# HGRN2 recurrence in a two-layer decoder trunk: 128-column products cut into two of 64, merged decays, a later output step

## The chip, the cores and the metric

The kernel runs on one NeuronCore of a Trainium2 chip. The metric is the device time of one execution in microseconds; a kernel's time is the median over its runs. TensorE multiplies into PSUM (128 partitions, banks of 512 float32 columns); VectorE (DVE in the profile), ScalarE (ACT) and GpSimd (POOL) do the rest; SyncE (SP) issues most transfers.

## The reference, cut to what matters

Two layers of a trunk at sequence length 256 and width 2048. Layer 0 holds a chunked gMLP beside an HGRN2 recurrence with 8 heads of 128, layer 1 an attention; a gated feed-forward follows each. The change touches the HGRN2 heads alone:

```python
def hgrn2(q, f_logit, i, g, lower_bound, o_gain):
    log_f = jnp.logaddexp(jnp.log(lb), jnp.log1p(-lb) + jax.nn.log_sigmoid(fl))
    k = (1.0 - lb) * jax.nn.sigmoid(-fl)
    ...
    def step(state, xs):
        q_c, k_c, v_c, lf_c = xs
        G = jnp.cumsum(lf_c, axis=2)
        o_inter = jnp.einsum('bhtk,bhkv->bhtv', q_c * jnp.exp(G), state)
        ...
        decay = jnp.exp(jnp.where(mask[:, :, None], diff, -jnp.inf))
        scores = jnp.einsum('bhtk,bhtsk,bhsk->bhts', q_c, decay, k_c)
        o_intra = jnp.einsum('bhts,bhsv->bhtv', scores, v_c)
        ...
    o = rms_norm(o, o_gain) * jax.nn.silu(g.astype(f32).reshape(shp))
```

For a pair of tokens t >= s, a head's score is the sum over features of q[t], k[s] and the product of the forget gates from s + 1 to t.

## The kernel before

All weights are streamed from HBM, split into two parts (`wh` on ScalarE, L168; `wl` on VectorE, L169) and multiplied in three matmuls a tile: L285 to L287 (`project_tok`), L259 and L262 (`project`), L304 to L306 (`project_four`). Everything between these products is written as generators. `tick()` (L121) is called once for each chunk of weights and moves every generator in flight on by one `yield`; up to `depth[0]` of them are in flight, three during the recurrence. So the order of the work is: a chunk of weights and its matmuls, then a step of each generator.

`mixer_ab` (L469) runs the projections of layer 0 one after another: v, f, then for each of 8 heads q (L750), with the values i in two groups of four heads (`values`, called ahead of heads 3 and 6), then the gates g and u. `gates` (L596) makes a head's forget gates `l` (128 features x 256 tokens; the second half of the tokens in reverse order) and keys `t[:, 0]`, `t[:, 1]`; L751 and L752 put the queries into `t[:, 3]` and `t[:, 2]`. Each head then runs `hgrn(h)` (L630):

- The diagonal of the scores: two products of 128 x 128 (L639), multiplied with an identity into the state tile `st` (L640). `st[:, 0]` holds the first 128 tokens' scores, `st[:, 1]` the last 128 tokens'.
- The levels (L648): for block widths n = 1, 2, 4, ... 64 from fine to coarse, ScalarE copies the decayed keys and queries into `E` (L652, two copies a level), then VectorE multiplies the even blocks (L656) and the odd blocks (L658) with the decay of their neighbour and folds the decays `tot` (L660). The last level (64) has only the even blocks.
- The scores of the levels: one product of 128 x 128 for each of the seven (L669), four into one PSUM bank and three into another, with the product between the two halves of the sequence (L673) between; VectorE copies each level's blocks into `st` under a mask (L682), after four levels and after the rest.
- The outputs, when the group's values exist (`itoks`): three products (L695 to L697), then a norm.

float32 products have two instructions each on TensorE. `tied` (L627) holds a product back until the matmul issued last by a projection; beyond that the instructions of an engine stand in an order that the framework chooses. PSUM tiles of the recurrence come from four banks (`px`).

Of the kernel before, what the change touches and what calls it, by code (L numbers as in the profile page):

```python
# [8 lines left out]
F32 = mybir.dt.float32  # L9
F32R = mybir.dt.float32r  # L10
U16 = mybir.dt.uint16
AF = mybir.ActivationFunctionType
ALU = mybir.AluOpType
AX = mybir.AxisListType

P = 128
S = 256
# [35 lines left out]
def tile_trunk(ctx: ExitStack, tc: tile.TileContext, x, pp_d, cst_d, mlev_d, msk_d,  # L53
# [13 lines left out]
    def nm(base):  # L67
        count[0] += 1
        return f"{base}_{count[0]}"
# [21 lines left out]
    def act(out_, in_, func, **kw):  # L91
        name = TABLE.get(func)
        if name is not None and name != epoch["set"]:
            ld = SC.preload_act_table_set(name)
            for o in epoch["ops"]:
                tc.add_manual_dep(ld.ins, o.ins.name, order, reason="table order")
            epoch.update(set=name, load=ld, ops=[ld])
        r = SC.activation(out_, in_, func, **kw)
        if name is not None:
            tc.add_manual_dep(r.ins, epoch["load"].ins.name, order, reason="table order")  # L100
            epoch["ops"].append(r)
        return r

    def view(ap, off, *dims):
        return bass.AP(ap.tensor, ap.offset + off, [list(ap.ap[0])] + [list(d) for d in dims])

    def back(ap):
        return view(ap, P - 1, (-1, P))
# [5 lines left out]
    def bank(tag="px"):  # L114
        n = nm(tag)
        return px.tile([P, 512], F32, tag=tag, name=n, bufs=banks[tag])

    banks = {"px": 4}
    flight, queue = [], []

    def tick():  # L121
        while queue and len(flight) < depth[0]:
            flight.append(queue.pop(0))
        for g in list(flight):
            if next(g, flight) is flight:
                flight.remove(g)
# [342 lines left out]
    def mixer_ab(norm):  # L469
# [126 lines left out]
        def gates(j, z):  # L596

            for _ in range(LAG):
                yield
            for i in range(4):  # L600
                l = keep("lf")
                t = hp.tile([P, 4, P], F32, tag="two", name=nm("kq"), bufs=2 * NH)
                first, second = view(z, i * S, (2, P)), view(z, (i + 1) * S - 1, (-2, P))
                held(act(l[:, 0:P], first, AF.Sigmoid))
                act(l[:, P:S], second, AF.Sigmoid)
                act(t[:, 0], first, AF.Sigmoid, scale=-1.0)
                act(t[:, 1], second, AF.Sigmoid, scale=-1.0)
                h = len(kq)
                V.tensor_scalar(t[:, 0:2], t[:, 0:2], omlb[:, h:h + 1], None, ALU.mult)
                lf.append(l)  # L610
                kq.append(t)
                yield
# [14 lines left out]
        def tied(r):  # L627
            tc.add_manual_dep(r.ins, deep["last"].ins.name, order, reason="not before")

        def hgrn(h):  # L630
            l, t = lf[h], kq[h]
            d0 = (h % 4) * P
            yield
            yield
            SC.activation(l, l, AF.Identity, bias=lb[:, h:h + 1], scale=omlb[:, h:h + 1])
            st = hp.tile([P, 2, P], F32, tag="st", name=nm("st"), bufs=3)
            dg = bank()
            for T in range(2):
                PE.matmul(dg[:, T * P:(T + 1) * P], t[:, T], t[:, 3 - T], start=True, stop=True)  # L639
            V.tensor_tensor(st, dg[:, 0:S].rearrange("p (a b) -> p a b", a=2),  # L640
                            ident.unsqueeze(1).to_broadcast([P, 2, P]), ALU.mult)
            yield

            V.tensor_tensor(t[:, 2:4], t[:, 2:4], view(l, P, (-P, 2), (1, P)), ALU.mult)
            E = hp.tile([P, NL, 2, P], F32, tag="E", name=nm("E"), bufs=2)
            tot = l
            tots = hp.tile([P, S], F32, tag="tot", name=nm("tot"), bufs=1)
            for li in reversed(range(NL)):  # L648
                n = LEVELS[li]
                m = P // n  # L650
                for sl in range(2):
                    SC.activation(E[:, li, sl].rearrange("p (b two n) -> p b two n", two=2, n=n),  # L652
                                  view(t, 2 * P * sl, (2 * n, 64 // n), (P + n, 2), (1, n)), AF.Copy)
                even = view(t, 0, (2 * P, 2), (2 * n, 64 // n), (1, n))
                odd = view(t, P + n, (2 * P, 2), (2 * n, 64 // n), (1, n))
                V.tensor_tensor(even, even, view(tot, 1, (m, 2), (2, m // 2), (0, n)), ALU.mult)  # L656
                if li:
                    V.tensor_tensor(odd, odd, view(tot, m, (-m, 2), (2, m // 2), (0, n)), ALU.mult)  # L658
                    nt = tots[:, S - 2 * m:S - m]
                    V.tensor_tensor(nt, view(tot, 0, (2, m)), view(tot, 1, (2, m)), ALU.mult)  # L660
                    tot = nt
                if n in (4, 16):
                    yield
            for _ in range(3):
                yield
            for c0, c1 in ((0, 4), (4, NL)):
                sps = bank()
                for li in range(c0, c1):
                    tied(PE.matmul(sps[:, (li - c0) * P:(li - c0 + 1) * P],  # L669
                                   E[:, li, 0], E[:, li, 1], start=True, stop=True))  # L670
                if c0 == 0:
                    xps = bank()
                    tied(PE.matmul(xps[:, 0:P], t[:, 0], t[:, 2], start=True, stop=True))  # L673
                    s128 = hp.tile([P, P], F32, tag="s128", name=nm("s128"), bufs=3)
                    SC.activation(back(s128), xps[:, 0:P], AF.Copy)
                for li in range(c0, c1):

                    n = LEVELS[li]
                    sv = view(st[:, 1], 0, (2 * n, 64 // n), (n - P, 2), (1, n))
                    m, d = (t_.rearrange("p (b two n) -> p b two n", two=2, n=n)  # L680
                            for t_ in (msk[:, li * P:(li + 1) * P], sps[:, (li - c0) * P:(li - c0 + 1) * P]))
                    V.copy_predicated(sv, m, d)  # L682
            s1 = hp.tile([P, P], F32, tag="s1", name=nm("s1"), bufs=2)
            SC.activation(back(s1), st[:, 1], AF.Copy)
            yield
            yield
            yield
            if len(itoks) <= h // 4:
                while len(itoks) <= h // 4:
                    yield  # L690
                yield
            itok = itoks[h // 4]
            op = bank()
            i0, i1 = (itok[:, T, d0:d0 + P] for T in range(2))
            tied(PE.matmul(op[:, 0:P], st[:, 0], i0, start=True, stop=True))  # L695
            tied(PE.matmul(op[:, P:S], s128, i0, start=True, stop=False))
            tied(PE.matmul(op[:, P:S], s1, i1, start=False, stop=True))  # L697
            so = hp.tile([P, LANE], F32, tag="so", name=nm("so"), bufs=2)[:, 0:2]
            ot = hp.tile([P, P], F32, tag="ot", name=nm("ot"), bufs=1)
            for T in range(2):  # L700
                SC.activation(ot, op[:, T * P:(T + 1) * P], AF.Square,
                              accum_out=so[:, T:T + 1])
            rsq(so, so, P)
            for T in range(2):
                SC.activation(os_[h // 4][:, T, d0:d0 + P], op[:, T * P:(T + 1) * P], AF.Copy,
                              scale=so[:, T:T + 1])
            left[0] -= 1
# [3 lines left out]
        def values(j):  # L711
            ps = project_tok(w_i[j], norm, lambda: hp.tile([P, 512], F32R, tag="ar", name=nm("ar"), bufs=2))
            itok = hp.tile([P, 2, 512], F32, tag="tok", name=nm("itok"), bufs=2)
            for T in range(2):
                SC.activation(itok[:, T], ps[T], AF.Copy, scale=Rr[:, T:T + 1])
            itoks.append(itok)

        silu = []

# [23 lines left out]
        for h in range(NH):  # L743
            if h in (3, 6):
                values(h // 4)
            while len(kq) <= h:
                tick()
            if h % 4 == 0:
                os_.append(hp.tile([P, 2, 512], F32, tag="o", name=nm("o"), bufs=2))
            z = fold(project(w_q[h], A))  # L750
            V.tensor_tensor(kq[h][:, 3], z[:, 0:P], R[:, 0:P], ALU.mult)  # L751
            V.tensor_tensor(back(kq[h][:, 2]), z[:, P:S], R[:, P:S], ALU.mult)  # L752
            queue.append(hgrn(h))
        for j in range(2):
            ps = project_four(w_g[4 * j:4 * j + 4], A, KT)
# [474 lines left out]
```

## Time and profile before

| | us |
|---|---|
| median of 3 runs (lowest to highest) | 2295.46 (2295.23 to 2295.96) |
| the profiled execution | 2295.65 |
| its span | 2293.9 |
| TensorE busy | 2288.2 |
| VectorE busy | 1566.4 |
| ScalarE busy | 1306.7 |
| GpSimd busy | 356.3 |

The profile shows each instruction with its engine, line and duration, groups of them by line, what an engine waited for, and the chain of work that ended last. PE is TensorE's matmuls and PEld its weight loads, which run beside the matmuls; matmul records overlap, so that a busy TensorE isn't one at its peak. Where a group is written `px<-E 128*128 128x128`, it reads tile `E`, writes a PSUM tile of pool `px`, uses 128 rows and 128 columns of the array, and moves 128 columns.

### The profile page before, as it was taken

To read this page: it belongs to the slowest core of one execution; us is meant where nothing else is said; L and a number is where in the kernel's file an instruction comes from. 1 tells how busy PE (TensorE), PEld (TensorE's weight loads), DVE (VectorE), ACT (ScalarE), POOL (GpSimd) and SP (SyncE) were. 2 spreads that over 40 slices of the span, in tenths; PEclk is the share of its full clock that TensorE was granted. 3 is DMA by queue.
4 is the path that set the end of the run, shared out by engine and by line. 5 is a ranking of instruction groups with operands and counts; after the bars stand their busy time and mean duration, and the time that the engine had idled before them with its cause. 6 is when DMAs were issued, how large, how long until landed. Compare 5 with 4: busy or idle time off the path is not lost.

```text
span 2293.9 us, 31385 instructions
## 1 busy us (share of the span) xinstructions
PE 2288.2 (100%) x10384; PEld 1902.4 (83%) x10384; DVE 1566.4 (68%) x2348; ACT 1306.7 (57%) x1964; POOL 356.3 (16%) x662
## 2 busy tenths in 40 slices
PE   9999999999999999999999999999999999999999
PEld 8888888888888888888888888888888888888887
DVE  7798767777566656766866665766776476657666
ACT  7676656665455545654555555655665465456642
POOL 0110212212012002111111101111211022012102
PEclk9999999999999999999999999999999999999999
DMA  8655677877667767776666656777777677667765
GB/s 290 197 156 157 196 217 226 242 214 229 199 206 218 213 200 210 221 216 187 211 222 202 194 178 179 224 221 235 228 223 215 194 215 211 211 202 218 222 203 174
DMA packets 489554, 480.38 MB, mean 209 GB/s; under 512 B 114128, under 2 KB 457184, under 8 KB 489392
## 3 DMA queue, kind: packets, MB, share of 16 engines
q1 hardware_dynamic: 467184, 453.54, 64.7%
q0 software_dynamic: 20480, 22.50, 4.4%
q10 hardware_dynamic: 1728, 2.35, 0.3%
q8 instruction: 81, 1.33, 0.3%
q14 instruction: 81, 0.66, 0.1%
HBM read 435.24 MB, written 2.11 MB: 191 GB/s over the span
## 4 chain that ended last, share of the span: by engine, by line
PE 98%; DMA 1%; DVE 1%; ACT 0%; issue 0%; SPq 0%; DVEq 0%; ACTq 0%
PE pm L305 26%; PE pm L304 26%; PE pm L306 26%; PE pm L285 4%; PE pm L286 4%; PE pm L287 4%; PE pm L259 2%; PE pm L186 1%; PE pm L262 1%; DMA w<-in_w_up 1%; PE pm L210 0%; PE px L669 0%; DVE wl L169 0%; PE px L888 0%; PE px L910 0%; ACT wh L168 0%
## 5 line engine op out<-in xcount | busy, mean ns | idle before, releaser
L169 DVE TENSOR_TENSOR wl<-w,wh 128x1024 fp32r<-128x1024 f32 (+1 forms) x820 | 996.0, 1218 | 630.3 <-ACT wh L168 620.7
L168 ACT ACTIVATE wh<-w 128x1024 fp32r<-128x1024 f32 (+1 forms) x820 | 862.3, 1054 | 791.4 <-PE pm L306 542.1
L304 PE MATMUL pm<-wh,a 128*128 128x512 f32 x1728 | 674.3, 390 | 0.0
L305 PE MATMUL pm<-wl,a 128*128 128x512 f32 x1728 | 672.6, 389 | 0.1
L306 PE MATMUL pm<-wh,a 128*128 128x512 f32 x1728 | 672.5, 389 | 0.0
L318 POOL DMA_DIRECT2D zt<-tmp x413 | 223.6, 549 | 1202.3 <-DVE tmp L313 1046.3
L305 PEld LDWEIGHTS pm<-wl,a 128*128 128x128 f32 x1728 | 324.4, 188 | 67.9 <-DVE wl L169 1.2
L306 PEld LDWEIGHTS pm<-wh,a 128*128 128x128 f32 x1728 | 324.3, 188 | 67.4
L304 PEld LDWEIGHTS pm<-wh,a 128*128 128x128 f32 x1728 | 324.4, 188 | 66.8
L304 PE MATMUL pm<-wh,hid 128*128 128x512 f32 x688 | 267.6, 389 | 0.0
L305 PE MATMUL pm<-wl,hid 128*128 128x512 f32 x688 | 267.6, 389 | 0.0
L306 PE MATMUL pm<-wh,hid 128*128 128x512 f32 x688 | 267.6, 389 | 0.0
L318 POOL DMA_DIRECT2D turn<-tmp x160 | 86.7, 550 | 506.3 <-DVE tmp L313 263.0
L285 PE MATMUL pm<-wh,a 128*128 128x512 f32 x416 | 165.2, 397 | 0.0
L287 PE MATMUL pm<-wh,a 128*128 128x512 f32 x416 | 162.2, 390 | 0.0
L286 PE MATMUL pm<-wl,a 128*128 128x512 f32 x416 | 162.0, 389 | 0.0
L306 PEld LDWEIGHTS pm<-wh,hid 128*128 128x128 f32 x688 | 129.1, 188 | 27.0
L304 PEld LDWEIGHTS pm<-wh,hid 128*128 128x128 f32 x688 | 129.1, 188 | 26.8
L305 PEld LDWEIGHTS pm<-wl,hid 128*128 128x128 f32 x688 | 129.1, 188 | 26.6
L1034 ACT ACTIVATE conv<-zt,pp 128x256 f32<-128x256 f32 x176 | 95.9, 589 | 26.2 <-DMA zt<-tmp 21.6
L313 DVE STREAM_TRANSPOSE tmp<-z 128x512 f32<-128x512 f32 x120 | 83.4, 704 | 19.4 <-ACT z L1020 18.7
L287 PEld LDWEIGHTS pm<-wh,a 128*128 128x128 f32 x416 | 78.1, 188 | 16.6
(241 smaller groups left out, 2097.7 us busy)
## 6 DMA issues: line engine op xcount, KB each, us to landing
w<-in_w_up SPq DMA_DIRECT2D x352, 512.0 KB, 4.5
w<-in_w_dn SPq DMA_DIRECT2D x176, 512.0 KB, 4.2
w<-in_w_cqkv SPq DMA_DIRECT2D x96, 512.0 KB, 4.4
w<-in_w_abo SPq DMA_DIRECT2D x32, 512.0 KB, 4.6
w<-in_w_cg SPq DMA_DIRECT2D x32, 512.0 KB, 4.3
w<-in_w_co SPq DMA_DIRECT2D x32, 512.0 KB, 4.6
zt<-tmp SPq DMA_DIRECT2D x414, 32.0 KB, 2.9
zt<-tmp POOLq DMA_DIRECT2D x413, 32.0 KB, 2.7
```

The source lines that it names most:

```text
L168: r = deep["wh"] = SC.activation(wh, w, AF.Copy)
L169: deep["wl"] = V.tensor_tensor(wl, w, wh.bitcast(F32), ALU.subtract)
L259: PE.matmul(ps, wh[:, k * P:(k + 1) * P], acts[done + k], start=done + k == 0, stop=False, skip_group_check=True)
L285: PE.matmul(ps[T], ah, h, start=k + i == 0, stop=False)
L286: PE.matmul(ps[T], ah, l, start=False, stop=False)
L287: deep["last"] = PE.matmul(ps[T], al, h, start=False, stop=k + i == KT - 1)
L304: PE.matmul(ps[T], ah, h, start=not begun and k + i == ks[0], stop=False)
L305: PE.matmul(ps[T], ah, l, start=False, stop=False)
L306: deep["mm"] = deep["last"] = PE.matmul(ps[T], al, h, start=False, stop=not more and k + i == ks[-1] + 1)
L313: V.transpose(tmp.rearrange("p (b m i t) -> p b m i t", b=4, m=4, t=2)[:, :, :, :, T], src(T).rearrange("p (m b j) -> p b m j", m=4, b=4))
L318: queues[(a + b) % len(queues)].dma_start(dst[BLK * b:BLK * (b + 1), :, a * n:(a + 1) * n], tmp[BLK * a:BLK * (a + 1), b * 4 * n:(b + 1) * ...
L1034: held(SC.activation(c, z, AF.Identity, bias=pp[:, cb:cb + 1], scale=w(2)))
```

## The change

- Diagonal and level products are each cut into two: rows 0 to 63 and 64 to 127 of the result, with 64 stationary and 64 moving columns each. A half is written into the upper or lower 64 PSUM partitions, and all seven levels now fit into one bank (7 x 64 columns). Blocks off the diagonal of 64, which no level below 64 needs, are no longer computed; level 64 takes the opposite column half.
- The masked copies become two a level, of 64 partitions and 64 columns each; level 64 is copied by ScalarE without a mask. The state tiles are three fixed ones whose never written quarters are set to zero once.
- The slots of `t` are permuted (keys in 0 and 3, queries in 2 and 1), so that the even blocks and the odd blocks of a level can be multiplied by one instruction of 256 elements instead of two of 128.
- A head's outputs are formed at the earliest two steps of `tick` after its values were made; before, a head that found them missing waited one step more, and one that found them went on at once.

```diff
+    steps = [0]
+
     def tick():
+        steps[0] += 1
...
-                act(t[:, 1], second, AF.Sigmoid, scale=-1.0)
+                act(t[:, 3], second, AF.Sigmoid, scale=-1.0)
                 h = len(kq)
-                V.tensor_scalar(t[:, 0:2], t[:, 0:2], omlb[:, h:h + 1], None, ALU.mult)
+                ks = view(t, 0, (3 * P, 2), (1, P))
+                V.tensor_scalar(ks, ks, omlb[:, h:h + 1], None, ALU.mult)
...
+        H = P // 2
+        sts = [hp.tile([P, 2, P], F32, tag=f"st{i}", name=f"st{i}") for i in range(3)]
+        for st in sts:
+            V.memset(st[H:P, 0, 0:H], 0.0)
+            V.memset(st[0:H, 1, H:P], 0.0)
...
-            st = hp.tile([P, 2, P], F32, tag="st", name=nm("st"), bufs=3)
+            st = sts[h % 3]
             dg = bank()
             for T in range(2):
-                PE.matmul(dg[:, T * P:(T + 1) * P], t[:, T], t[:, 3 - T], start=True, stop=True)
-            V.tensor_tensor(st, dg[:, 0:S].rearrange("p (a b) -> p a b", a=2),
-                            ident.unsqueeze(1).to_broadcast([P, 2, P]), ALU.mult)
+                for r in (0, H):
+                    PE.matmul(dg[r:r + H, T * H:(T + 1) * H], t[:, 3 * T, r:r + H], t[:, 2 - T, r:r + H],
+                              start=True, stop=True)
+            for r in (0, H):
+                V.tensor_tensor(st[r:r + H, :, r:r + H], dg[r:r + H, 0:P].rearrange("p (a b) -> p a b", a=2),
+                                ident[r:r + H, r:r + H].unsqueeze(1).to_broadcast([H, 2, H]), ALU.mult)
...
+                    two = P + n if sl else 3 * P + n
                     SC.activation(E[:, li, sl].rearrange("p (b two n) -> p b two n", two=2, n=n),
-                                  view(t, 2 * P * sl, (2 * n, 64 // n), (P + n, 2), (1, n)), AF.Copy)
-                even = view(t, 0, (2 * P, 2), (2 * n, 64 // n), (1, n))
-                odd = view(t, P + n, (2 * P, 2), (2 * n, 64 // n), (1, n))
-                V.tensor_tensor(even, even, view(tot, 1, (m, 2), (2, m // 2), (0, n)), ALU.mult)
+                                  view(t, P * sl, (2 * n, 64 // n), (two, 2), (1, n)), AF.Copy)
                 if li:
-                    V.tensor_tensor(odd, odd, view(tot, m, (-m, 2), (2, m // 2), (0, n)), ALU.mult)
+                    both = view(t, 0, (2 * P + n, 2), (2 * n, P // n), (1, n))
+                    V.tensor_tensor(both, both, view(tot, 1, (-1, 2), (2, m), (0, n)), ALU.mult)
...
+                else:
+                    even = view(t, 0, (P, 2), (1, n))
+                    V.tensor_tensor(even, even, view(tot, 1, (m, 2), (0, n)), ALU.mult)
...
-            for c0, c1 in ((0, 4), (4, NL)):
-                sps = bank()
-                for li in range(c0, c1):
-                    tied(PE.matmul(sps[:, (li - c0) * P:(li - c0 + 1) * P],
-                                   E[:, li, 0], E[:, li, 1], start=True, stop=True))
-                if c0 == 0:
-                    xps = bank()
-                    tied(PE.matmul(xps[:, 0:P], t[:, 0], t[:, 2], start=True, stop=True))
...
-                for li in range(c0, c1):
...
-                    V.copy_predicated(sv, m, d)
+            sps = bank()
+            for li in range(NL):
+
+                for r in (0, H):
+                    c = r if li else H - r
+                    tied(PE.matmul(sps[r:r + H, li * H:(li + 1) * H], E[:, li, 0, r:r + H], E[:, li, 1, c:c + H],
+                                   start=True, stop=True))
+            xps = bank()
+            tied(PE.matmul(xps[:, 0:P], t[:, 0], t[:, 1], start=True, stop=True))
+            s128 = hp.tile([P, P], F32, tag="s128", name=nm("s128"), bufs=3)
+            SC.activation(back(s128), xps[:, 0:P], AF.Copy)
+            for li in range(NL):
+
+                n = LEVELS[li]
+                for r in (0, H):
+                    d = sps[r:r + H, li * H:(li + 1) * H]
+                    if li == 0:
+                        SC.activation(st[r:r + H, r // H, H - r:P - r], d, AF.Copy)
+                        continue
+                    sv = view(st[r:r + H, 1], r, (2 * n, 32 // n), (n - P, 2), (1, n))
+                    m = msk[r:r + H, li * P + r:li * P + r + H]
+                    V.copy_predicated(sv, *(t_.rearrange("p (b two n) -> p b two n", two=2, n=n) for t_ in (m, d)))
...
-            if len(itoks) <= h // 4:
-                while len(itoks) <= h // 4:
-                    yield
-                yield
-            itok = itoks[h // 4]
+            while len(itoks) <= h // 4 or steps[0] < itoks[h // 4][1] + 2:
+                yield
+            itok = itoks[h // 4][0]
...
-            itoks.append(itok)
+            itoks.append((itok, steps[0]))
...
-            V.tensor_tensor(kq[h][:, 3], z[:, 0:P], R[:, 0:P], ALU.mult)
-            V.tensor_tensor(back(kq[h][:, 2]), z[:, P:S], R[:, P:S], ALU.mult)
+            V.tensor_tensor(kq[h][:, 2], z[:, 0:P], R[:, 0:P], ALU.mult)
+            V.tensor_tensor(back(kq[h][:, 1]), z[:, P:S], R[:, P:S], ALU.mult)
```

More of the change, by code (lines that the diff above doesn't have):

```diff
@@ L635, in hgrn @@
             SC.activation(l, l, AF.Identity, bias=lb[:, h:h + 1], scale=omlb[:, h:h + 1])
-            st = hp.tile([P, 2, P], F32, tag="st", name=nm("st"), bufs=3)
+            st = sts[h % 3]
             dg = bank()
             for T in range(2):
-                PE.matmul(dg[:, T * P:(T + 1) * P], t[:, T], t[:, 3 - T], start=True, stop=True)
-            V.tensor_tensor(st, dg[:, 0:S].rearrange("p (a b) -> p a b", a=2),
-                            ident.unsqueeze(1).to_broadcast([P, 2, P]), ALU.mult)
+                for r in (0, H):
[4 more added lines that the diff above has]
+                                ident[r:r + H, r:r + H].unsqueeze(1).to_broadcast([H, 2, H]), ALU.mult)
             yield
-            V.tensor_tensor(t[:, 2:4], t[:, 2:4], view(l, P, (-P, 2), (1, P)), ALU.mult)
+            V.tensor_tensor(t[:, 1:3], t[:, 1:3], view(l, P, (-P, 2), (1, P)), ALU.mult)
             E = hp.tile([P, NL, 2, P], F32, tag="E", name=nm("E"), bufs=2)
@@ L665, in hgrn @@
                 yield
-            for c0, c1 in ((0, 4), (4, NL)):
-                sps = bank()
-                for li in range(c0, c1):
-                    tied(PE.matmul(sps[:, (li - c0) * P:(li - c0 + 1) * P],
-                                   E[:, li, 0], E[:, li, 1], start=True, stop=True))
-                if c0 == 0:
-                    xps = bank()
-                    tied(PE.matmul(xps[:, 0:P], t[:, 0], t[:, 2], start=True, stop=True))
-                    s128 = hp.tile([P, P], F32, tag="s128", name=nm("s128"), bufs=3)
-                    SC.activation(back(s128), xps[:, 0:P], AF.Copy)
-                for li in range(c0, c1):
[L678 to L682, printed above, removed]
+            sps = bank()
[18 more added lines that the diff above has]
+                    V.copy_predicated(sv, *(t_.rearrange("p (b two n) -> p b two n", two=2, n=n) for t_ in (m, d)))
             s1 = hp.tile([P, P], F32, tag="s1", name=nm("s1"), bufs=2)
```

## The prediction

> **What bounds the kernel now.** I read the page first: engine shares, then the chain that ended last. TensorE is busy throughout the span and 98% of the chain is its own matmuls, so an edit counts if it changes how long TensorE's stream is, or makes that stream wait.
>
> ```profile
> span 2293.9 us, 31385 instructions
> PE 2288.2 (100%) x10384; PEld 1902.4 (83%) x10384; DVE 1566.4 (68%) x2348; ACT 1306.7 (57%) x1964; POOL 356.3 (16%) x662
> PE 98%; DMA 1%; DVE 1%; ACT 0%; issue 0%; SPq 0%; DVEq 0%; ACTq 0%
> ```
>
> The profiled execution took 2295.65 us, 1.75 more than its span and 0.19 more than the median of the three runs, 2295.46. I sum against 2295.65 and take 0.19 off at the end.
>
> The recurrence lies between about 105 and 245 us. There VectorE is busy 118.25 of 140 us (84%), against 56.75 of 85 (67%) just after: it is the one engine besides TensorE with little room.
>
> ```profile
> core 0: us, PE busy (x) PEld busy (x) DVE busy (x) ACT busy (x) POOL busy (x), PEclk, DMA share, GB/s
> 105.00:245.00 140.00, 139.25 (x767) 119.86 (x766) 118.25 (x319) 98.30 (x268) 14.94 (x28) 1.00 0.52 159
> 245.00:330.00 85.00, 85.00 (x377) 70.38 (x376) 56.75 (x78) 53.47 (x70) 17.32 (x32) 1.00 0.76 226
> ```
>
> Next, the groups by line in that stretch and TensorE's waits. The products that change are L639 (diagonal) and L669 (levels), 32 + 112 instructions over eight heads: 18 a head, two for each of 2 + 7 products. Matmul records overlap, so their busy time is not their cost; that is the spacing of starts.
>
> ```profile
> L669 PE MATMUL px<-E 128*128 128x128 f32 x112 | 15.2, 276 | 0.5 <-ACT E L652 0.5
> L639 PE MATMUL px<-kq 128*128 128x128 f32 x32 | 4.9, 274 | 0.0
> PE px L669 <- ACT E L652: 0.5, 1, 0.5
> PE px L697 <- ACT itok L715: 0.2, 1, 0.2
> ```
>
> The timeline of TensorE (start, duration, instruction) gives the spacing, for the bursts of the first two heads and the first outputs:
>
> ```profile
> 128.40 0.39 PE L287 MATMUL pm<-wh,ar 128*128 128x512 f32 x1
> 128.62 1.05 PE L669 MATMUL px<-E 128*128 128x128 f32 x8
> 129.51 0.39 PE L673 MATMUL px<-kq 128*128 128x128 f32 x2
> 129.74 0.83 PE L669 MATMUL px<-E 128*128 128x128 f32 x6
> 130.32 0.48 PE L285 MATMUL pm<-wh,a 128*128 128x512 f32 x1
> 130.64 0.40 PE L286 MATMUL pm<-wl,a 128*128 128x512 f32 x1
> 130.87 0.39 PE L287 MATMUL pm<-wh,a 128*128 128x512 f32 x1
> ...
> 133.37 0.39 PE L286 MATMUL pm<-wl,a 128*128 128x512 f32 x1
> 134.30 1.16 PE L669 MATMUL px<-E 128*128 128x128 f32 x8 [0.55 <-ACT E L652]
> ...
> 142.02 0.71 PE L259 MATMUL pm<-a,wh 128*128 128x512 f32 x2
> 142.94 0.49 PE L697 MATMUL px<-itok,s 128*128 128x128 f32 x2 [0.21 <-ACT itok L715]
> 143.18 0.48 PE L262 MATMUL pm<-a,wl 128*128 128x256 f32 x2
> ```
>
> Eight level instructions take 129.51 - 128.62 = 0.89 us, 0.111 each; six and one wide matmul take 130.64 - 129.74 = 0.90, which with 0.23 for the wide one (130.87 - 130.64) is 0.112 each. So a head's 18 cost 2.02 us of stream and all heads 16.1: nothing done to these products can save more than 0.7% of the time.
>
> **The products, two of 64 columns.** Each of the nine becomes two with 64 stationary and 64 moving columns: 36 instructions a head. No row has that shape; the nearest give its size:
>
> ```profile
> L669 PEld LDWEIGHTS px<-E x112: 186/192/192, 128.4 to 230.6; 128*128 128x128 f32 x112
> L669 PE MATMUL px<-E x112: 270/275/377, 128.6 to 230.7; 128*128 128x128 f32 x112
> L888 PE MATMUL px<-qk x32: 379/380/382, 1176.6 to 1410.8; 128*128 128x256 f32 x32
> L844 PEld LDWEIGHTS pm<-a,w x16: 147/148/149, 1147.8 to 1151.2; 128*80 128x80 f32 x16
> ```
>
> 128 moving columns more cost 380 - 275 = 105 ns, or 52 for 64. 48 stationary columns fewer save 192 - 148 = 44 ns, or 59 for 64. Both sides shrink with the columns, so a half costs about 112 - 52 = 60 ns of stream when it stands alone. One after another, 36 x 0.060 = 2.16 us against 2.02: +0.14 a head, +1.1 us in all. That is one end. At the other end a head's upper and lower halves, which own different columns of the array and different partitions of PSUM, run side by side: 36 x 0.030 = 1.08 us, -0.94 a head, -7.5 in all. A third bound, beyond these: if a half costs a whole instruction's 0.112, +2.02 a head, +16.1 us; the row of 80 columns speaks against it, since a narrower load is shorter there. I take the side-by-side end: the records show TensorE already holding a matmul of 0.275 us while it starts the next after 0.112, so what limits it is the columns it streams and loads, not the instruction's length; -7.5 us.
>
> The Trainium skill, "TensorE: Matmul & The Clock Gate", section Part 3: Packing small matmuls — row/col tiling, says that products put at different output partitions land in different column groups and run concurrently (2.38 times for three of 32 columns). By it the term would be the same -7.5 us; no run here shows it yet.
>
> **Going into and out of the halves.** Each head has two runs of halves (4 products of the diagonal, 14 of the levels) between wide matmuls: 16 runs, 32 changes. If a change is free, 0: in the timeline the step from a wide matmul (128.40) to the first level product (128.62) is 0.22, no dearer than the next wide one. If nothing may be in flight or loaded ahead across it, the wide matmul ends 0.39 - 0.23 = 0.16 after its slot, and the load of the next weights is then exposed:
>
> ```profile
> 128.40 1.08 PEld L669 LDWEIGHTS px<-E 128*128 128x128 f32 x8
> ```
>
> It starts at 128.40 for a matmul at 128.62, 0.22 ahead. So the upper end is 0.38 a change, 12.2 us in all. I take a value in between, an estimate from the stream alone: the load itself can't be done ahead, 0.06 us going in (64 columns) and 0.112 coming out: 0.17 a run, +2.75 us.
>
> The Trainium skill, "TensorEngine Tiling (Array Packing)", section Key Properties, has a rule against this change: a change of the tiling mode drains TensorE. It gives no price; no run here shows one.
>
> **Vector and scalar work.** Durations from these rows (min/median/max in ns):
>
> ```profile
> L656 DVE TENSOR_TENSOR kq<-kq,tot x48: 280/291/530, 115.2 to 226.8; 128x128 f32<-128x128 f32 x48
> L658 DVE TENSOR_TENSOR kq<-kq,tot x40: 270/284/489, 115.4 to 225.9; 128x128 f32<-128x128 f32 x40
> L644 DVE TENSOR_TENSOR kq<-kq,lf x8: 409/415/417, 112.4 to 211.6; 128x256 f32<-128x256 f32 x8
> L640 DVE TENSOR_TENSOR st<-px,cst x8: 410/416/647, 112.0 to 211.3; 128x256 f32<-128x256 f32 x8
> L682 DVE COPY_PREDICATED st<-msk,px x56: 292/302/762, 130.5 to 233.3; 128x128 f32<-128x128 uint16 x56
> L675 ACT ACTIVATE s<-px x8: 249/254/283, 131.3 to 230.7; 128x128 f32<-128x128 f32 x8
> ACT E L652 <- DVE kq L658: 16.9, 18, 1.8
> ```
>
> The decays: six levels lose 291 + 284 and gain one of 415 (L644's 256 elements), -0.96 us a head; level 64 keeps its one. 128 elements more cost 415 - 284 = 131 ns, so 64 fewer save 66. The masked copies go from 7 of 302 to 12 of about 236, +0.72; the diagonal from one of 416 to two of about 285, +0.15. VectorE's net is -0.09 us a head: nothing, between -1.3 (narrow ones shrink to half: -0.96 + 12 x 0.151 - 2.11) and +1.0 (they don't shrink at all: -0.96 + 5 x 0.302 + 0.42). ScalarE gets two small copies of level 64, about 0.2 us each (L675 less 64 elements), 3.2 us in all; it has 42 of 140 us free. It also waits less: the 16.9 us for L658 shrink as each level's two products become one. The six fills of the fixed state tiles, the moved slots of queries and keys, and the strided view in the gates cost at most six times 0.29, 1.7 us of VectorE, once, ahead of the recurrence, and no DMA is added, removed or moved.
>
> The cover for all this is the lead that VectorE has over TensorE with the weights' low halves (L169):
>
> ```profile
> 127.66 1.22 DVE L169 TENSOR_TENSOR wl<-w,wh 128x1024 fp32r<-128x1024 f32 x1
> ...
> 243.29 0.19 PEld L305 LDWEIGHTS pm<-wl,a 128*128 128x128 f32 x1 [0.21 <-DVE wl L169]
> ```
>
> The half done at 127.66 + 1.22 = 128.88 is first used by the matmul at 133.37, 4.5 us later; but at 243.29 the lead is gone and the load waits 0.21 us. The masked copies now wait for all 14 products, the plain product and ScalarE's two copies out of the same bank, where they used to start after four levels; behind them on VectorE stand the next low halves, behind ScalarE's copies the high ones. That is at most about 2 us later a head (1.6 us burst and two copies), inside a lead of 4.5. A shorter stream also uses the lead up: 118.25 us of VectorE in some 135 is 88%. Cost taken: +0.5 us; bounds 0 and 8 x 1 us.
>
> **The outputs.** A head that meets its values in the very step after they were made now waits one more. The first head did: its last product waited for ScalarE's copy, and 142.94 comes 0.92 after 142.02 where two wide matmuls take 0.46: -0.46 us. Other heads that had been waiting already went on two steps after, so nothing else moves; what is late is one head's outputs by one step, long before the gates need all of a group. The stall of the second head's levels (134.30 - 133.37 less 0.23: 0.70 us) hangs on the chain of decays and copies, which gets shorter while TensorE arrives sooner: I count half, -0.35; bounds 0 and -0.70.
>
> **Sum.** -7.5 + 2.75 + 0.5 - 0.46 - 0.35 = -5.06 us: 2290.6 for the profiled execution, 2290.4 for the median.
>
> **Rivals.** A, halves one after another, changes free: +1.1 + 0.5 - 0.8 = +0.8, 2296.3. For it: no row shows two matmuls side by side.
> B, the other side: each change lets the array run empty. With halves one after another and 0.2 to 0.38 a change it is +6.4 to +12.2 on top of A, 2303 to 2308; with halves side by side it only eats the gain. It makes the kernel slower by more than 0.2% from about 0.12 us a change on (0.8 + 32 x 0.12 = 4.6) where the halves don't overlap. For it: 32 changes in a stream without gaps; against: the step into L669 costs nothing extra today. The tiling page's rule of the Trainium skill, above, points to B's mechanism.
> C, the gain turns into waits for low halves: VectorE keeps its 118 us, the lead falls to zero as at 243.29, and TensorE gives back 1 us in three or four heads: 2290.4 + 3.5 = 2294.
> D, side by side with free changes: 2290.4 - 2.75 = 2287.7, or 2286.8 if the second stall goes in full and VectorE costs nothing.
>
> **How the numbers follow.** A measurement of this kernel can tell about 0.2%, 4.6 us, from no change: faster is below 2290.9. Chances: forecast 0.36 (2288.5 to 2292.5; of it 0.26 under 2290.9), D 0.18, A 0.14, C 0.08, B and a half that costs more than 0.06 us 0.24 (2300 and up). Faster 0.26 + 0.18 = 0.44, same 0.10 + 0.14 + 0.08 = 0.32, slower 0.24. The range 2286 to 2303 takes in A, C, D and the lower part of B, and leaves out some 0.16: the two highest ends (a whole slot a half, full drains).
>
> **What would show it.** Side by side: starts of a head's 28 level instructions spread over some 0.85 us, not 1.7. The price of a change: the step from the last wide matmul before a run to its first half, and from the last half to the next wide one, against 0.22 and 0.23. Stalls: the waits of L669 and L697 gone, those of low halves still under 1 us. A burst of 28 that lasts 1.6 us or more, or steps of 0.4 at its ends, proves the forecast wrong.

## The result and the profile after

The changed kernel takes 2299.4 us (median of 20 runs, 2299.07 to 2300.7) against 2295.53 us (20 runs, 2294.79 to 2296.0) before: a ratio of 1.0018, 95% interval 1.0011 to 1.0024. It is 3.9 us slower, where 5.1 us faster was forecast. The engines' shares and the chain that ended last, of the changed kernel's page:

```profile
span 2297.7 us, 31703 instructions
PE 2286.6 (100%) x10528; PEld 1896.3 (83%) x10528; DVE 1572.4 (68%) x2354; ACT 1309.3 (57%) x1980; POOL 357.5 (16%) x662
PE 94%; DVE 3%; ACT 1%; issue 1%; DMA 0%; SPq 0%; DVEq 0%; ACTq 0%
```

And its busy time in the recurrence's stretch and in the one behind it (PE, PEld, DVE, ACT, POOL as before):

```profile
105.00:245.00 140.00, 135.02 (x901) 111.66 (x900) 120.23 (x315) 97.00 (x276) 15.55 (x28) 1.00 0.52 158
245.00:330.00 85.00, 83.90 (x369) 68.90 (x368) 57.43 (x79) 55.63 (x78) 17.32 (x32) 1.00 0.73 217
```

TensorE's records cover 135.02 of the 140 us, 139.25 before: it now stands idle. The loss falls in this stretch: the same matmul comes 4.2 us later than in the kernel before at 246 us, and still 4.2 later at 800. VectorE and ScalarE have entered the chain that ended last, 3% and 1%. The gain is there to be seen as well. The changed kernel's timeline of TensorE, first a run of level halves, then one of diagonal halves:

```profile
128.75 0.39 PE L290 MATMUL pm<-wh,ar 128*128 128x512 f32 x1
129.06 1.03 PE L687 MATMUL px<-E 128*64 128x64 f32 x28
130.03 0.49 PE L690 MATMUL px<-kq 128*128 128x128 f32 x2
130.27 0.48 PE L288 MATMUL pm<-wh,a 128*128 128x512 f32 x1
130.59 0.39 PE L289 MATMUL pm<-wl,a 128*128 128x512 f32 x1
...
138.46 0.39 PE L290 MATMUL pm<-wh,ar 128*128 128x512 f32 x1
138.78 0.45 PE L651 MATMUL px<-kq 128*64 128x64 f32 x8
139.16 0.50 PE L288 MATMUL pm<-wh,a 128*128 128x512 f32 x1
139.50 0.40 PE L289 MATMUL pm<-wl,a 128*128 128x512 f32 x1
```

28 halves of 0.22 us each are through in 130.03 - 129.06 = 0.97 us. In the trace they start in pairs, the two of a pair 0.007 us apart and the pairs 0.058: the halves run side by side. But the steps at the ends are longer. From the wide matmul ahead to the second one behind, levels and plain product take 130.59 - 128.75 = 1.84 us; before, 130.64 - 128.40 = 2.24. That is 0.40 us won a head. The diagonal takes 139.50 - 138.46 = 1.04; the same stretch before took 0.90:

```profile
138.25 0.39 PE L287 MATMUL pm<-wh,ar 128*128 128x512 f32 x1
138.48 0.60 PE L639 MATMUL px<-kq 128*128 128x128 f32 x4
138.84 0.48 PE L285 MATMUL pm<-wh,a 128*128 128x512 f32 x1
139.15 0.40 PE L286 MATMUL pm<-wl,a 128*128 128x512 f32 x1
```

0.14 us lost a head: eight halves and their changes cost more than the two whole products. The other heads give the same, where nothing waits: 0.40 to 0.41 won, 0.13 to 0.14 lost. Together 0.26 us a head, 2.1 us in all, is all that TensorE's stream gained.

What it lost stands in TensorE's waits, here those of the changed kernel (total, times, longest) that the kernel before did not have:

```profile
PE px L690 <- DVE kq L677: 2.8, 3, 1.3
PE pm L265 <- DVE wl L172: 1.4, 1, 1.4
...
PE pm L289 <- DVE wl L172: 0.8, 1, 0.8
PE pm L308 <- DVE wl L172: 0.8, 1, 0.8
PE pm L307 <- ACT wh L171: 0.3, 1, 0.3
```

The plain product (L690) waits three times for the last decay, the projections three times for a low half of the weights and once for a high half: 6.1 us idle. One of each in the timeline, and what VectorE did ahead of the first:

```profile
134.87 1.04 PE L687 MATMUL px<-E 128*64 128x64 f32 x28
137.23 0.46 PE L690 MATMUL px<-kq 128*128 128x128 f32 x2 [1.33 <-DVE kq L677]
...
190.78 0.61 PE L262 MATMUL pm<-a,wh 128*128 128x512 f32 x2
192.76 0.51 PE L265 MATMUL pm<-a,wl 128*128 128x256 f32 x2 [1.37 <-DVE wl L172]
```

```profile
134.19 2.58 DVE L703 COPY_PREDICATED st<-msk,px 64x64 f32<-64x64 uint16 x8
136.79 0.29 DVE L677 TENSOR_TENSOR kq<-kq,tot 128x128 f32<-128x128 f32 x1
```

Eight masked copies of the head ahead (L703) stand on VectorE in front of the decay (L677) that the second head's plain product needs: TensorE waits for the copies. At 190.78 the two wide matmuls would have taken 0.47 us; they took 1.98, so a wait costs some 0.14 more than the idle time that is shown. The account of the spans, 2293.9 to 2297.7: -2.1 (stream), -0.46 (the outputs' wait, gone), -0.6 (the second head's stall of levels: 134.87 follows the wide matmul ahead by the usual step into a run), +6.1 idle and about +1 for seven such refills, an estimate from this one: +3.9; measured +3.8.

### The profile page after: what moved, and what is told of

It reads as the page before. It is cut to its first block, busy times and chain, and to the rows that moved or that the text cites. A ratio compares the mean times of both kernels' runs of the same rounds, so it can differ in the third digit from the quotient of the medians.

```text
span 2297.7 us, 31703 instructions
## 1 busy us (share of the span) xinstructions
PE 2286.6 (100%) x10528; PEld 1896.3 (83%) x10528; DVE 1572.4 (68%) x2354; ACT 1309.3 (57%) x1980; POOL 357.5 (16%) x662
## 4 chain that ended last, share of the span: by engine, by line
PE 94%; DVE 3%; ACT 1%; issue 1%; DMA 0%; SPq 0%; DVEq 0%; ACTq 0%
PE pm L309 26%; PE pm L308 26%; PE pm L307 26%; PE pm L288 4%; PE pm L289 4%; PE pm L290 4%; PE pm L189 1%; DVE st L703 1%; DVE wl L172 1%; PE pm L262 1%; DVE kq L671 1%; PE pm L213 0%; ACT wh L171 0%; PE pm L265 0%; PE px L907 0%
## 5 line engine op out<-in xcount | busy, mean ns | idle before, releaser
L307 PEld LDWEIGHTS pm<-wh,a 128*128 128x128 f32 x1728 | 324.4, 188 | 67.5 <-ACT wh L171 0.8
L309 PEld LDWEIGHTS pm<-wh,a 128*128 128x128 f32 x1728 | 324.4, 188 | 67.3
L289 PE MATMUL pm<-wl,a 128*128 128x512 f32 x416 | 162.1, 390 | 0.8 <-DVE wl L172 0.8
L1054 DVE SCALAR_TENSOR_TENSOR conv<-zt,pp,conv 128x255 f32<-128x255 f32 x176 | 78.3, 477 | 21.3 <-ACT conv L1053 16.6
```

Of the source, the lines that this page charges most:

```text
L289: PE.matmul(ps[T], ah, l, start=False, stop=False)
L307: PE.matmul(ps[T], ah, h, start=not begun and k + i == ks[0], stop=False)
L309: deep["mm"] = deep["last"] = PE.matmul(ps[T], al, h, start=False, stop=not more and k + i == ks[-1] + 1)
L1054: V.scalar_tensor_tensor(c[:, 1:], z[:, :S - 1], w(1), c[:, 1:], ALU.mult, ALU.add)
```

## The experiments

Theory 1: the masked copies are what makes VectorE late. Twelve small ones take longer than seven large ones, and behind them wait decays, low halves and, on ScalarE, the copy of the finished state. Theory 2: any shorter stream would use up VectorE's lead; the copies don't matter. Theory 3: the outputs' new step gathers two heads' outputs. Theory 4: the copies are late because all wait for one bank's fourteen products. Each run was taken beside runs of the kernel before (medians 2294.96 to 2295.34).

**The copies left out** (of the changed kernel; the scores of six levels are then missing from its result):

```diff
...
-                    V.copy_predicated(sv, *(t_.rearrange("p (b two n) -> p b two n", two=2, n=n) for t_ in (m, d)))
```

> The changed kernel with the twelve masked copies of each head (levels 32 to 1) left out, so these scores are missing from the result. Theory 1 (VectorE falls behind because the copies, at 0.27 us one after another, cost a head 3.3 us instead of 2.3): most of the 13.6 us of extra spacing on TensorE go, 2288 us or less, and the plain product waits no more for the last decay. Theory 2 (a stream that is 8 us shorter uses up the lead by itself, whatever the copies cost): at least 6 us of extra spacing remain, 2293 or more.

Measured: 2292.41 us, ratio to before 0.9989 (0.9979 to 0.9998). 7.0 us of the changed kernel's time go. The number of theory 1 is missed all the same: it took the stream's gain to be 8 us, and the stream's gain is 2.1. With that, worked out afterwards, 2295.2 - 2.1 - 1.1 (the two old stalls) is 2292.0. Theory 2 (2293 or more) fell short too: a stream as short as this one, without the copies, has hardly a wait, one of 0.4 us.

**The outputs' step undone**

```diff
-            while len(itoks) <= h // 4 or steps[0] < itoks[h // 4][1] + 2:
-                yield
+            if len(itoks) <= h // 4:
+                while len(itoks) <= h // 4:
+                    yield
+                yield
```

> The changed kernel with the outputs' step as before. Theories 1 and 2: the time stays within 1 us of the changed kernel's 2299.4, at most 0.5 us slower for the first head's wait for its values. Theory 3 (two heads' outputs in one step push VectorE and ScalarE behind): faster by 2 us or more.

Measured: 2299.35 us. The first head's wait for its values is back, 0.8 us, and the total is the same: in its trace the changed kernel's wait of 0.8 us at L289 for a low half is gone. A wait in one place gives VectorE time that it otherwise takes later. Theory 3 falls.

**The decays alone on the kernel before** (slots permuted, L656 and L658 merged)

```diff
...
-                V.tensor_tensor(even, even, view(tot, 1, (m, 2), (2, m // 2), (0, n)), ALU.mult)
...
                 if li:
-                    V.tensor_tensor(odd, odd, view(tot, m, (-m, 2), (2, m // 2), (0, n)), ALU.mult)
+                    both = view(t, 0, (2 * P + n, 2), (2 * n, P // n), (1, n))
+                    V.tensor_tensor(both, both, view(tot, 1, (-1, 2), (2, m), (0, n)), ALU.mult)
```

> The kernel before with the permuted slots and the merged decays alone: products, copies and outputs as before. VectorE saves 6 times (2 x 0.207 - 0.343) = 0.4 us a head. Theory 1: no slower than before, 2295.0 to 2295.7. Rival: the larger instruction lengthens the chain of copies and decays, slower by 1 us or more.

Measured: 2294.85 us, ratio 0.9999 (0.9990 to 1.0009): no difference that can be told. Theory 1 had it no slower; the rival, slower by 1 us or more, falls.

**The decays undone in the changed kernel**

```diff
-                    both = view(t, 0, (2 * P + n, 2), (2 * n, P // n), (1, n))
-                    V.tensor_tensor(both, both, view(tot, 1, (-1, 2), (2, m), (0, n)), ALU.mult)
+                    even = view(t, 0, (2 * n, P // n), (1, n))
+                    odd = view(t, 2 * P + n, (2 * n, P // n), (1, n))
+                    V.tensor_tensor(even, even, view(tot, 1, (2, m), (0, n)), ALU.mult)
+                    V.tensor_tensor(odd, odd, view(tot, 0, (2, m), (0, n)), ALU.mult)
```

> The changed kernel with two products a level for the decays, as before, on the permuted slots. VectorE does 6 x (2 x 0.207 - 0.343) = 0.4 us a head more. Theory 1: slower than the changed kernel by 1 to 4 us, 2300 to 2303. Rival (the decays are off the path of the stalls): the same within 0.5 us.

Measured: 2301.93 us, ratio 1.0031 (1.0018 to 1.0044), 2.5 us above the changed kernel; its five runs scatter more than the others, 2300.34 to 2303.99. The same 0.4 us of VectorE a head is worth nothing on the kernel before and 2.5 us here: here VectorE is on the path.

**The copies alone on the kernel before**

```diff
-                    V.copy_predicated(sv, m, d)
+                    H = P // 2
+                    for r in (0, H) if li else (None,):
...
+                        sv = view(st[rows, 1], o, (2 * n, w // (2 * n)), (n - P, 2), (1, n))
...
+                        V.copy_predicated(sv, m, d)
```

> The kernel before with one part alone: the masked copies of levels 32 to 1 each cut into two of 64 partitions and 64 columns, twelve a head; products, banks, decays, outputs as before. TensorE's stream is unchanged. Theory 1 (the copies' number delays VectorE, and ScalarE behind it): slower by 2 to 8 us, 2297 to 2303, with new waits for low halves or for decays. Theory 2 (the shorter stream uses up the lead) and theory 4 (what delays is that all copies now wait for one bank's fourteen products): no change within 1 us of before.

Measured: 2302.01 us, ratio 1.0030 (1.0019 to 1.0042): 6.7 us slower with TensorE's products, the banks and the order of reads untouched. Theories 2 and 4 had this at no change. The group of the masked copies between 105 and 245 us (count | busy us, mean ns | idle before), first in the kernel before, then in this one:

```profile
L682 DVE COPY_PREDICATED st<-msk,px 128x128 f32<-128x128 uint16 x56 | 21.4, 383 | 2.2 <-PE px L669 1.1
```

```profile
L687 DVE COPY_PREDICATED st<-msk,px 64x64 f32<-64x64 uint16 x96 | 26.5, 276 | 2.9
```

And two waits of this one:

```profile
ACT s L689 <- DVE st L687: 16.1, 8, 4.2
...
PE px L700 <- ACT itok L720: 2.6, 2, 1.9
```

The six cut levels are 96 instructions where they were 48, and the group's busy time rises from 21.4 to 26.5 us although its eight whole copies of level 64 are now counted elsewhere: two half copies come to 552 ns on average where a whole one came to 383. The group holds different durations, here in the changed kernel (min/median/max in ns; below it twelve in a row):

```profile
L703 DVE COPY_PREDICATED st<-msk,px x96: 214/233/456, 132.7 to 239.0; 64x64 f32<-64x64 uint16 x96
235.83 3.67 DVE L703 COPY_PREDICATED st<-msk,px 64x64 f32<-64x64 uint16 x12
239.53 1.22 DVE L172 TENSOR_TENSOR wl<-w,wh 128x1024 fp32r<-128x1024 f32 x1
```

Eight of a head's twelve last 0.21 to 0.24 us, the two of blocks of two columns 0.29 to 0.30 and the two of single columns 0.42 to 0.46: 0.275 on average. Whole copies differ alike: 0.30, then 0.44 and 0.73. In the row of twelve each starts 0.03 us after the end of the one ahead: 239.53 - 235.83 = 3.70 us, 0.31 each. In the kernel before, 33 of the 56 whole copies were followed by another kind of instruction, which started 0.10 us (median) before the copy's end; in the changed kernel 85 of the 96 are followed by another copy. So, counted from start to start, seven whole copies held VectorE for 2.2 us a head and twelve halves hold it for 3.7.

ScalarE's copy of the state waits for the last of them, eight times; in the kernel with the copies alone these eight waits come to 16.1 us, before they were four with 5.1. Behind that copy stand the next high halves and the values, for which TensorE waits (L700). In all TensorE waits 5.3 us in the kernel with the copies alone, 0.9 before (the wait at the start left out); some 1 to 2 us of the 6.7 stand in no wait and were not traced.

**ScalarE's copy of the state one step later**

```diff
+            yield
             s1 = hp.tile([P, P], F32, tag="s1", name=nm("s1"), bufs=2)
             SC.activation(back(s1), st[:, 1], AF.Copy)
-            yield
             yield
             yield
```

> The changed kernel with ScalarE's reversed copy of the last state half given out one step later, so that ScalarE does not wait in its queue for the twelve masked copies (16.9 us in all). Theory 1a (VectorE's own time for the copies is what is late): 2297 or more. Theory 1b (ScalarE's wait passes on to the weights' high halves, and through them to the low ones): 2294 or less.

Measured: 2298.55 us, 0.85 below the changed kernel. The time is theory 1a's, but the edit separates the two less than it was meant to: ScalarE still waits 11.1 us for the copies, of 16.9, and TensorE still for decays and halves. How much of the loss is VectorE's own time and how much goes by way of ScalarE's queue is not settled.

**Six copies over 128 partitions.** The two halves of a level lie in the same 64 columns of PSUM. If the destination is a tile `sd` of 64 columns too, with a mask of the same shape, one instruction does a level and one the diagonal; ScalarE spreads `sd` into the state tile with two copies.

```diff
+            V.tensor_tensor(sd, dg[:, 0:P].rearrange("p (a b) -> p a b", a=2),
+                            idc.unsqueeze(1).to_broadcast([P, 2, H]), ALU.mult)
...
+                sv = view(sd[:, 1], 0, (2 * n, 32 // n), (n - H, 2), (1, n))
+                V.copy_predicated(sv, *(t_.rearrange("p (b two n) -> p b two n", two=2, n=n)
+                                        for t_ in (mc[:, li], sps[:, li * H:(li + 1) * H])))
+            for r in (0, H):
+                SC.activation(st[r:r + H, :, r:r + H], sd[r:r + H], AF.Copy)
```

> The changed kernel with the diagonal and the levels 32 to 1 gathered in a tile of 64 columns, so that one masked copy of 128 partitions does a level (6 instead of 12 a head) and one instruction the diagonal; ScalarE spreads the tile into the state tile with two copies; state tiles two instead of three. Theory 1: VectorE saves about 6 x 0.27 + 0.3 = 1.9 us a head against the changed kernel, most stalls go, 2288 to 2291. Theory 2: TensorE still waits for the low halves, 2294 or more.

Measured: 2294.53 us, ratio 0.9997 (0.9988 to 1.0007). Every new wait of TensorE was gone, yet the time missed theory 1's band. Compared matmul by matmul, the stream was 2.3 us ahead of the kernel before at 246 us; between 308 and 382 us it lost 1.9 again, evenly, with no wait. There the stationary tiles come from the pool whose layout the smaller mask (896 bytes a partition, before 1792) should have shifted; the traces hold no addresses. So the mask was padded:

```diff
-        mc = hp.tile([P, NL, P // 2], U16, tag="msk", name="mc")
+        mc = hp.tile([P, NL + 1, P // 2], U16, tag="msk", name="mc")[:, 0:NL]
```

> The kernel with six copies over 128 partitions, its mask tile padded from 896 to 1024 bytes, so that every later tile of the pool starts at a multiple of 256 bytes again. In the unpadded one TensorE's stream lost 2 us evenly between 308 and 382 us, where its stationary tiles come from that pool. If the offset is the cause: 2 to 3 us faster than that kernel's 2294.5, 2291 to 2292. If not: the same within 0.5 us.

Measured: 2292.07 us, ratio 0.9986 (0.9977 to 0.9995), 2.5 us below the unpadded one. TensorE's groups between 308 and 382 us, unpadded first, then padded:

```profile
L308 PE MATMUL pm<-wl,ya 128*128 128x512 f32 x59 | 23.3, 395 | 0.0
```

```profile
L308 PE MATMUL pm<-wl,ya 128*128 128x512 f32 x61 | 23.7, 389 | 0.0
```

The same matmuls last 395 ns instead of 389, so 6 ns, and some 330 of them follow one another in that stretch: 2 us.

**The offset alone on the kernel before**

```diff
-        msk = hp.tile([P, NL * P], U16, tag="msk", name="msk")
+        msk = hp.tile([P, NL * P + 64], U16, tag="msk", name="msk")[:, 0:NL * P]
```

> The kernel before with its mask tile 128 bytes longer and nothing else, so that the later tiles of the pool start 128 bytes off a multiple of 256. If the offset of the stationary tiles slows TensorE's stream: 2 to 3 us slower, 2297.5 to 2298.5, with wide matmuls 0.233 us apart between 308 and 382 us instead of 0.227. If not: the same.

Measured: 2297.72 us, ratio 1.0011 (1.0003 to 1.0020): 2.8 us for 128 bytes that nothing reads. Compared matmul by matmul, 1.9 of them are lost between 308 and 382 us again, where its matmuls too last 395 ns.

**The diagonal whole again**, on the padded kernel:

```diff
             for T in range(2):
-                for r in (0, H):
-                    PE.matmul(dg[r:r + H, T * H:(T + 1) * H], t[:, 3 * T, r:r + H], t[:, 2 - T, r:r + H],
-                              start=True, stop=True)
+                PE.matmul(dg[:, T * P:(T + 1) * P], t[:, 3 * T], t[:, 2 - T], start=True, stop=True)
...
```

> The same as the padded kernel with six copies, but the diagonal's products as before, two of 128 columns, read out by two VectorE instructions of 64 partitions instead of one. It has 16 changes between wide matmuls and halves instead of 32. From the spacing in the changed kernel a run of eight halves with its two changes takes 0.59 us, two whole products 0.45: 1.1 us faster than the padded kernel if TensorE's stream decides; VectorE does 0.3 us more a head, so equal or slower if VectorE decides.

Measured: 2291.11 us, ratio 0.9983 (0.9974 to 0.9992), 1.0 below the padded kernel where 1.1 was expected from the spacing. It is the fastest of all, 4.2 us below the kernel before and 8.3 below the changed one. Its copies between 105 and 245 us take half of the changed kernel's time, since one over 128 partitions lasts as long as one over 64 did, 275 ns, and none of its waits on TensorE lies in the recurrence:

```profile
L700 DVE COPY_PREDICATED sd<-mc,px 128x64 f32<-128x64 uint16 x48 | 13.2, 275 | 1.0
```

**The price of the changes by itself**: the kernel before with four more instructions of halves a head, whose result nobody reads.

```diff
+            for r in (0, P // 2):
+                PE.matmul(dg[r:r + P // 2, S:S + P // 2], t[:, 0, 0:P // 2], t[:, 3, 0:P // 2], start=True, stop=True)
```

> The kernel before with one more run of halves a head: behind the diagonal's products two of 64 columns into a part of the bank that nobody reads. The price of the changes alone: in the changed kernel a run pays about 0.09 us going in and 0.12 + 0.12 coming out beside its halves at 0.03 each. Theory (0.33 us a run, four instructions): +0.45 us a head, 3.6 us in all, 2298.5 to 2299.5. Rival (a change costs what I took, 0.17 a run): +2.3 us. Rival (free): +1.

Measured: 2299.94 us, ratio 1.0022 (1.0014 to 1.0031), 5.0 us. An undisturbed run in its timeline of TensorE:

```profile
139.91 0.39 PE L287 MATMUL pm<-wh,ar 128*128 128x512 f32 x1
140.14 0.60 PE L639 MATMUL px<-kq 128*128 128x128 f32 x4
140.67 0.34 PE L641 MATMUL px<-kq 128*64 128x64 f32 x4
140.94 0.50 PE L285 MATMUL pm<-wh,a 128*128 128x512 f32 x1
141.27 0.40 PE L286 MATMUL pm<-wl,a 128*128 128x512 f32 x1
```

141.27 - 139.91 = 1.36 us, 0.90 without the halves: 0.46 a run, of which 0.12 for four halves at 0.03 and 0.34 for going in and out. All eight runs cost the same, 3.7 us together. The profiled execution, the longest of the eleven (2301.45 us), has a span 5.7 us longer than before; there TensorE also waits 2.3 us where it waited 0.9 (the wait at the start left out). What makes the median 1.3 us longer than the 3.7 was not traced further.

## Why the prediction was wrong

- **Halves side by side, -7.5 us: right.** 0.97 us for 28, the way out included, where 0.84 (28 x 0.030) was taken. The rule of the Trainium skill ("TensorE: Matmul & The Clock Gate", Part 3: Packing small matmuls — row/col tiling) agrees with the trace: the two halves of a pair start 0.007 us apart.
- **The changes, +2.75 us: the mechanism right, the size half of it.** 0.17 us a run was taken, 0.32 to 0.34 measured: in the changed kernel two wide slots (0.45), the plain product (0.22) and 28 halves at 0.03 (0.84) are 1.52 of the 1.84 us, which leaves 0.32; measured alone it is 0.34. Over 16 runs that is 5.3 us, inside the bounds 0 and 12.2. The rule of the Trainium skill ("TensorEngine Tiling (Array Packing)", Key Properties), that a change of the tiling mode drains TensorE, fits these 0.32 us a run. Alone, this term would have left the forecast at about -2.5.
- **Vector work at nothing, hidden by the lead, +0.5 us: the step that failed.** It was "VectorE's net is -0.09 us a head: nothing", behind a lead of 4.5 us. What it cost TensorE is 6.1 us of idle time and, by the estimate above, about 1 of refills. The sum was made of durations of single instructions, and what an instruction holds the engine for is the time to the next start. A decay of 128 elements lasts 0.29 us and costs about 0.21, since the next one starts inside it, so the merge saved 0.4 us a head and not 0.96. The copies were put at +0.72 from medians (302 to 236 ns; 302 and 233 measured, but 383 and 275 on average); from start to start they cost 3.7 - 2.2 = +1.5. The diagonal's two instructions cost 0.2 more, as was taken. The net is some +1.3 us a head, over the bound of +1.0. And the place matters: a head's twelve copies stand between the decays and the weights of an engine that was 84% busy. The bound given for the cost, 8 x 1 us, would have held all of it, and the 6.7 that the copies alone cost.
- **The outputs' step, -0.46: right in the trace, worth nothing in the total**, since the undone step gives the same time.
- **The second head's stall, -0.35:** it is gone as a wait of the levels and came back as a wait of the plain product, 1.3 us at 137 us.
- **The rivals.** C (the gain turns into waits for VectorE) names the engine that decided, but not the reason: the lead was lost to the copies, not to the shorter stream, which has no wait in the recurrence with six copies a head; and the waits came to 6.1 us, 3.0 of them for low halves, not 3.5. A did not come about, since the halves overlap, nor D, since the changes cost. Of B the price came about nearly, 0.16 us a change where it asked for 0.2 to 0.38, but with halves side by side it only ate the gain.
- **The range.** That 2299.4 us lies between 2286 and 2303 is luck: the upper end was there for halves one after another with dear changes, not for waits on VectorE.

## What to carry to other kernels

Price work on a busy in-order engine by the spacing of starts in the order in which they will stand, not by their durations, take the mean and not the median where a group mixes lengths, and look at what stands behind the block; cutting an instruction in two halves its elements, not its cost. A layout that helps TensorE has to be read out at its own width: the same products gain 3.3 us with six copies (the padded kernel) and lose 3.9 with twelve. Runs of small tiled matmuls pay for each change in and out, so gather them into few long runs and leave short ones whole.

## What was not expected of the hardware

Matmuls of 128x64 in alternating column halves started 0.03 us apart on average, where one of 128x128 took 0.112, and a run of them cost 0.32 to 0.34 us at its ends. A masked copy of 64 columns lasted 275 ns on average over 64 partitions and over 128, and 0.44 us instead of 0.23 where its blocks were single columns. A tile 128 bytes longer, which by the tiles' sizes puts the pool's later tiles 128 bytes off a multiple of 256, made matmuls with stationary operands from that pool 6 ns longer (395 against 389) and the kernel 2.8 us, with no wait that a profile names.
